# Up projection of a decoder layer: 18 seven-product steps instead of 16, four of them in each of two column groups

## The chip, the core and the metric

The kernel runs on one core of one Trainium2 chip. The metric is the device time of one execution in microseconds (us); lower is better. The core's engines work side by side, each with its own queue in fixed order: TensorE (PE, with its weight loads PEld) multiplies matrices into banks of PSUM, VectorE (DVE) and ScalarE (ACT) do elementwise work, GpSimd (POOL) and SyncE (SP) mostly issue transfers here. They wait for one another by semaphores.

## What is computed

One layer of a decoder trunk on 256 tokens of width 2048, all in float32: a mixer (mLSTM and attention heads), a gated feed-forward network, and a gated side input. The change concerns only the first product of the feed-forward network, the up projection:

```
h = rms_norm(x, ffn_norm_g)
u = h @ w_up                      # 256 x 2048 times 2048 x 11264
a, g = jnp.split(u, 2, axis=-1)   # 5632 columns each
a = causal_dwconv(a, conv_w, conv_b)
x = x + (jax.nn.gelu(a, approximate=False) * g) @ w_down
```

## The kernel before, in words

**One product.** TensorE takes each float32 operand as two rounded parts, a high part and a low rest, and forms high x high, high x low and low x high: three matmuls of 128 x 128 by 128 x 512 (`three`, lines 365 to 367). The left operand is the transposed, normed x (`x2`), kept in SBUF in both parts. The weights stream in from HBM once, and each block is split on the chip: ScalarE casts the high part (line 1296), VectorE subtracts it for the low one (line 1298).

**Column groups.** The up projection runs over 11 column groups q = 0 to 10 (`up_group`, line 1699), each of 512 columns of a and the same 512 of g. A group goes over 16 blocks k of 128 rows of the weights. A plain block ("p") is two halves of tokens by two halves of columns, four products, 12 matmuls, into four banks.

**Sevens.** Two blocks and the two halves of tokens make a 2 by 2 matrix product of blocks, which needs eight products as written and seven by the scheme of Strassen and Winograd. The kernel calls this a seven ("a" for the first pair of blocks of a group, "b" for the second). It comes as four units of 1, 2, 2 and 2 products (3, 6, 6, 6 matmuls, 21 instead of 24). For it VectorE forms four sums of weight halves ahead of the splits (lines 1743, 1744, 1754, 1755), and the sums of the left operand are made once for each pair of blocks (`up_sums`, line 1792) and kept in `S_up`. Four products go straight to the group's banks or to banks of their own (`pb`, tile name upP); at the last seven of a group four steps (lines 1765 to 1768) combine those banks into `z_up`, which is added to the group's rows later.

**The order of a group** is written out by hand as a string (`ORDERS`, line 48), one letter for each unit:

```
ORDERS = ("pppppp" "apapapap" "bpbbbp",
          *("pppppp" "apapapap" "pppp", "ppp" "apapapap" "bpbpbpb" "pp") * 4,
          *("pppppp" "apapapap" "pppp",) * 2)
```

So group 0 has two sevens, groups 1 to 8 have one and two in turn, groups 9 and 10 have one: 16 in all. `START[q]` is the index of a group's first unit.

**After a group.** Its four banks are scaled into `EZ` (`up_rows`, line 1154). Then, in the course of the next group: `up_turn` (line 1156) adds `z_up` (line 1161, twice) and transposes 32 x 32 squares into `Y` (line 202, twice), and 16 transfers on POOL and SP bring the squares back to `EZ` in place (line 208). `up_act` (line 1174) does ten steps: four scalings for the convolution (lines 1180 and 1183, ScalarE), two shifted sums (line 1187), GELU (line 1190), the gate (line 1193), the split into two parts (lines 158 and 159), and for some groups the left sums of the down projection (lines 470 to 474). `TURN_AT` and `ACT_AT` say behind which unit of the next group each step is queued, at the earliest.

**Lead and buffers** (`run_units`, line 1304). The queues of all engines are filled unit by unit. Before the matmuls of unit i are queued, loads are queued as long as a raw buffer is free, and splits for the units up to i + `AHEAD_UP` - 1 (4 ahead) as long as split buffers are free. There are eight raw buffers of 512 KB (raw0 to raw2, v0 to v4) and eight split buffers (four high, four low); a unit takes two split buffers, the first unit of a seven one. Buffers come back when TensorE has read them. The framework then lays down each engine's order from these queues and may move an instruction that has nothing to wait for ahead of one that has.

**Banks.** PSUM has four banks under each of two names, mm and aux. Even groups use mm for their rows and aux for their sevens; odd groups have aux for their rows and mm for their sevens.

Of the kernel before, what the change touches and what calls it, by code (L numbers as in the profile page):

```python
# [9 lines left out]
F32 = mybir.dt.float32  # L10
# [5 lines left out]
P = 128  # L16
S = 256
NT = S // P
# [6 lines left out]
KF = FF // P  # L25
# [8 lines left out]

BLK = 1024
RAW, PARTS = 3, 4
AHEAD_UP, AHEAD_LATE = 4, 6

SEVEN = (2, 4, 6, 8, 10, 12, 14, 16, 18)
FIRST = (0, 1, 2, 3, 5, 7, 4, 9, 6, 11, 8, 13, 10, 15, 12, 17, 14, 19, 16, 20, 18, 21)  # L40
# [4 lines left out]
FRONT = (8, 4, 4)  # L45
SEVENS_UP = 2
UP_K = (4, 5, 6, 7, 0, 1, 2, 3, 8, 9, 10, 11, 12, 13, 14, 15)
ORDERS = ("pppppp" "apapapap" "bpbbbp",
          *("pppppp" "apapapap" "pppp", "ppp" "apapapap" "bpbpbpb" "pp") * 4,
          *("pppppp" "apapapap" "pppp",) * 2)  # L50
START = [sum(map(len, ORDERS[:q])) for q in range(12)]
TURN_AT = (-1, -1, 0, 0)
GATE_ORDER = "ppppp" "apapapap" "bpbpbb" "p"
OUT_K = (8, 9, 10, 11, 12, 13, 14, 15, 0, 1, 2, 3, 4, 5, 6, 7)
OUT_ORDERS = ("pppp" "apapapap" "bpbpbpb" "p", "pp" "apapapa" "bpbpbb" "ppppp")
ACT_AT = (9, 10, 11, 12, 13, 14, 15, 16, 17, 18)


@with_exitstack
def layer_kernel(  # L60
# [29 lines left out]
    def f32(ap):  # L90
        return ap.bitcast(F32)
# [375 lines left out]
    def sums_of(u, f, t):  # L467

        a11, a12 = u[:, 0, 0:P], u[:, 1, 0:P]
        dve.tensor_sub(f[:, 1::2], u[:, 0].rearrange("p (i c) -> p i c", c=P), u[:, :, P:S])  # L470
        dve.tensor_sub(f[:, 0], f[:, 3], a11)
        dve.tensor_add(f[:, 2], a12, f[:, 0])
        act.copy(t[:, :, 0:P], f)
        dve.tensor_sub(t[:, :, P:256], f, f32(t[:, :, 0:P]))
# [30 lines left out]
    with mixers:  # L505
# [416 lines left out]
        at = len(blocks)  # L922
# [13 lines left out]
        def with_after(b, hook):  # L936
            fn = b.fn
            b.fn = lambda hi, lo: (fn(hi, lo), hook())
# [153 lines left out]
    with tc.tile_pool(name="ffn", bufs=1) as fp:  # L1092
# [4 lines left out]
        uB = fp.tile([P, 8, 512], F32R, tag="uB", name="uB")  # L1097
        uC = fp.tile([P, 8, 512], F32R, tag="uC", name="uC")
        S_up = [fp.tile([P, 4, 256], F32R, tag=f"u{42 - 2 * r}", name=f"S_up{r}") for r in range(SEVENS_UP)]
        spare_raws = {k: fp.tile([P, 2, BLK], F32, tag=k, name=f"{k}r") for k in ("u32", "u36")}  # L1100
        ends = {}

# [50 lines left out]

            act.activation(EZ[:, t, n * 512 : (n + 1) * 512], b, AF.Copy, scale=r2["t"][:, t : t + 1])

        def up_turn():

            y = Y.rearrange("p (t b c) -> p t b c", t=NT, b=4)

            def summed(t):  # L1160
                return lambda: dve.scalar_tensor_tensor(
                    out=EZ[:, t], in0=xs[:, 1, t * BLK : (t + 1) * BLK], scalar=r2["t"][:, t : t + 1], in1=EZ[:, t],
                    op0=ALU.mult, op1=ALU.add)

            def turned(t):
                def f():
                    square(y, t, 0, EZ[:, t])
                    if t == NT - 1:
                        with tc.issue_after(last["load"]):
                            move(y, Z, nc.sync)  # L1170
                return f
            return [f(t) for t in range(NT) for f in (summed, turned)]

        def up_act(q):

# [30 lines left out]

        late = {}
        now = [0]
        spaces = [f"raw{i}" for i in range(RAW)] + [f"{k}{i}" for k in ("hi", "lo") for i in range(PARTS)] + ["v0", "v1", "v2", "v3", "v4"]
        until = {"v0": 8, "v1": 8, "v2": 9, "v3": 9}  # L1210
        splits = (*spaces[RAW : RAW + 2 * PARTS], "w0", "w1", "w2", "w3")
        held, used = set(), {}
        for j in range(done[0] - PARTS, done[0]):
            used[f"hi{j % PARTS}"] = used[f"lo{j % PARTS}"] = used[f"raw{j % RAW}"] = len(used)
# [89 lines left out]
        def run_units(us, first_late, gate):  # L1304
            loaded = split = 0
            for i, u in enumerate(us):
                if i == first_late:
# [391 lines left out]
        def up_group(q):  # L1699
# [1 line left out]
            w = w_up[0].rearrange("(k p) (h c) -> k p h c", p=P, h=2)  # L1701
            st = {}

            n7 = "a" in ORDERS[q], "b" in ORDERS[q]
            first, n7 = 2 * sum(n7), sum(n7)
# [83 lines left out]
            kinds = {"p": iter(us), "a": iter(seven(0)), "b": iter(seven(1))}  # L1789
            return [next(kinds[c]) for c in ORDERS[q]]  # L1790

        def up_sums(r):
            k = UP_K[2 * r]
            f, d = (EZ[:, 0, i * 512 : (i + 1) * 512].rearrange("p (k c) -> p k c", c=256) for i in range(2))
            dve.tensor_add(f, f32(x2[:, k : k + 2, 0:256]), f32(x2[:, k : k + 2, 256:512]))
            sums_of(f, EZ[:, 1, 0:512].rearrange("p (i c) -> p i c", i=4), S_up[r])

        us = []
        for q in range(KF // 4):
# [2 lines left out]
        for i in range(4):  # L1802
            with_after(us[6 + 2 * i], between(lambda i=i: keep_x(4 + i)))
        with_after(us[3], between(lambda: r2.update(t=rstd_of(ssq2, "ffn"))))
        for r, i in enumerate((2, 9)):
            with_after(us[i], between(lambda r=r: up_sums(r)))
        for i, k0 in enumerate(range(8, KD, 2)):
            with_after(us[1 + i], behind(lambda k0=k0: transpose_x(x2, k0, g_ffn)))
# [16 lines left out]
            at = len(g_) // 2  # L1825
            us += g_[:at] + p_ + g_[at:]
        for q in range(KF // 4):
            for job, i in zip(up_turn(), TURN_AT if q < KF // 4 - 1 else (-1, 0, -1, 1)):
                with_after(us[START[q + 1] + i], between(job))
            for i, job in enumerate(up_act(q)):  # L1830
                if q < KF // 4 - 1:
                    with_after(us[START[q + 1] + ACT_AT[i]], between(job))
# [35 lines left out]
```

## Time and profile before

| | us |
|---|---|
| median of 3 runs | 1230.20 |
| lowest, highest | 1229.74, 1230.36 |
| the profiled execution | 1230.42 |
| span of its instructions | 1228.7 |

Busy time in the span: TensorE 1222.4, its weight loads 1029.6, VectorE 1010.1, ScalarE 757.2, GpSimd 179.7. The granted clock of TensorE is 0.999 on average.

A profile is one execution recorded by the hardware. Its page gives busy times, the chain of work that ended last and the costliest groups of instructions by line; the trace behind it answers questions: windows (busy time of each engine in a stretch), a timeline, groups by line and shape, and who waited for whom. "L1298" is line 1298 of the kernel. In a row such as "part<-raw" the tile written stands left and those read stand right. A number in square brackets is the idle time of the engine just before the instruction, with what ended it. Matmuls are pipelined, so single durations overlap and the distance from start to start is what one costs.

### The profile page before, as it was taken

To read this page: it belongs to the slowest core of one execution; us is meant where nothing else is said; L and a number is where in the kernel's file an instruction comes from. 1 tells how busy PE (TensorE), PEld (TensorE's weight loads), DVE (VectorE), ACT (ScalarE), POOL (GpSimd) and SP (SyncE) were. 2 spreads that over 40 slices of the span, in tenths; PEclk is the share of its full clock that TensorE was granted. 3 is DMA by queue.
4 is the path that set the end of the run, shared out by engine and by line. 5 is a ranking of instruction groups with operands and counts; after the bars stand their busy time and mean duration, and the time that the engine had idled before them with its cause. 6 is when DMAs were issued, how large, how long until landed. Compare 5 with 4: busy or idle time off the path is not lost.

```text
span 1228.7 us, 16419 instructions
## 1 busy us (share of the span) xinstructions
PE 1222.4 (99%) x5589; PEld 1029.6 (84%) x5589; DVE 1010.1 (82%) x1262; ACT 757.2 (62%) x1109; POOL 179.7 (15%) x331
## 2 busy tenths in 40 slices
PE   9999999999999999999999999999999999999998
PEld 7999988888888888888888888888888888888887
DVE  6788857675679989888998898998788999999773
ACT  7567545565655665766676676757657556556652
POOL 2011237243401401011101101110110000050000
PEclk9999999999999999999999999999999999999999
DMA  9566687676565787777687678756797896876570
GB/s 307 179 197 194 176 228 223 184 216 194 164 234 181 232 262 231 241 220 240 201 275 242 185 250 271 224 173 222 240 313 247 304 360 200 269 251 210 198 225 35
DMA packets 128869, 276.37 MB, mean 225 GB/s; under 512 B 14777, under 2 KB 26545, under 8 KB 128785
## 3 DMA queue, kind: packets, MB, share of 16 engines
q1 hardware_dynamic: 117392, 257.40, 65.9%
q0 software_dynamic: 11008, 17.76, 5.1%
q8 instruction: 44, 0.72, 0.2%
q14 instruction: 40, 0.33, 0.1%
q10 hardware_dynamic: 385, 0.16, 0.1%
HBM read 247.99 MB, written 8.93 MB: 209 GB/s over the span
## 4 chain that ended last, share of the span: by engine, by line
PE 99%; DMA 0%; SPq 0%; DVE 0%; ACT 0%; issue 0%; DVEq 0%
PE up L367 12%; PE up L365 12%; PE up L366 12%; PE tg L355 6%; PE tg L354 6%; PE tg L356 6%; PE pg L365 5%; PE pg L366 5%; PE pg L367 5%; PE dnP L1347 1%; PE dnP L1348 1%; PE dnP L1346 1%; PE upP L367 1%; PE upP L366 1%; PE upP L365 1%; PE gt L367 1%
## 5 line engine op out<-in xcount | busy, mean ns | idle before, releaser
L366 PE MATMUL up<-part,x2T 128*128 128x512 f32 x608 | 236.5, 389 | 0.0
L367 PE MATMUL up<-part,x2T 128*128 128x512 f32 x608 | 236.1, 390 | 0.0
L1296 ACT CAST part<-raw 128x1024 fp32r<-128x1024 f32 (+1 forms) x144 | 145.6, 1021 | 113.6 <-PE up L367 35.7
L300 DVE TENSOR_TENSOR lo<-raw,hi 128x1024 fp32r<-128x1024 f32 (+3 forms) x119 | 139.1, 1171 | 76.3 <-ACT hi L298 75.9
L365 PE MATMUL up<-part,x2T 128*128 128x512 f32 x608 | 185.9, 389 | 0.0
L1298 DVE TENSOR_TENSOR part<-raw,part 128x1024 fp32r<-128x1024 f32 (+1 forms) x140 | 164.1, 1179 | 23.4 <-ACT part L1296 17.1
L298 ACT CAST hi<-raw 128x1024 fp32r<-128x1024 f32 (+3 forms) x119 | 120.1, 1011 | 96.3 <-PE tg L356 44.9
L365 PEld LDWEIGHTS up<-part,x2T 128*128 128x128 f32 x608 | 114.2, 188 | 23.6
L366 PEld LDWEIGHTS up<-part,x2T 128*128 128x128 f32 x608 | 114.2, 188 | 23.6
L367 PEld LDWEIGHTS up<-part,x2T 128*128 128x128 f32 x608 | 114.0, 188 | 23.5
L356 PE MATMUL tg<-hi,hT 128*128 128x512 f32 x288 | 113.6, 395 | 0.0
L355 PE MATMUL tg<-lo,hT 128*128 128x512 f32 x288 | 113.3, 393 | 0.0
L354 PE MATMUL tg<-hi,hT 128*128 128x512 f32 x288 | 112.4, 396 | 0.0
L208 POOL DMA_DIRECT2D EZ<-Y x66 | 35.1, 539 | 364.3 <-issue 204.7
L1296 ACT CAST part<-u36r 128x1024 fp32r<-128x1024 f32 (+1 forms) x46 | 47.8, 1042 | 34.6 <-PE up L367 18.9
L1298 DVE TENSOR_TENSOR part<-u36r,part 128x1024 fp32r<-128x1024 f32 (+1 forms) x46 | 55.5, 1206 | 9.8 <-ACT part L1296 5.4
L355 PEld LDWEIGHTS tg<-lo,hT 128*128 128x128 f32 x288 | 54.1, 188 | 11.1 <-DVE lo L300 0.3
L356 PEld LDWEIGHTS tg<-hi,hT 128*128 128x128 f32 x288 | 54.1, 188 | 10.9
L354 PEld LDWEIGHTS tg<-hi,hT 128*128 128x128 f32 x288 | 53.8, 188 | 10.8
L1298 DVE TENSOR_TENSOR part<-u32r,part 128x1024 fp32r<-128x1024 f32 (+1 forms) x44 | 50.2, 1145 | 13.4 <-ACT part L1296 10.3
L1296 ACT CAST part<-u32r 128x1024 fp32r<-128x1024 f32 (+1 forms) x44 | 43.3, 991 | 22.7 <-PE up L367 9.0
L366 PE MATMUL pg<-lo,hT 128*128 128x430 f32 (+1 forms) x156 | 55.7, 357 | 0.0
(936 smaller groups left out, 2767.4 us busy)
## 6 DMA issues: line engine op xcount, KB each, us to landing
raw<-in_w_up_dram SPq DMA_DIRECT2D x78, 512.0 KB, 4.9
raw<-in_w_in_dram SPq DMA_DIRECT2D x71, 512.0 KB, 4.4
u36r<-in_w_up_dram SPq DMA_DIRECT2D x43, 512.0 KB, 5.2
raw<-in_w_down_dram SPq DMA_DIRECT2D x41, 512.0 KB, 5.6
u32r<-in_w_up_dram SPq DMA_DIRECT2D x34, 512.0 KB, 4.9
xs<-in_w_up_dram SPq DMA_DIRECT2D x21, 512.0 KB, 4.8
w2b<-in_w_down_dram SPq DMA_DIRECT2D x20, 512.0 KB, 5.9
raw<-in_w_out_dram SPq DMA_DIRECT2D x17, 512.0 KB, 4.8
```

The source lines that it names most:

```text
L208: (other if other and (4 * a + b) % 3 else pool).dma_start(out=c[32 * b : 32 * b + 32, a::4], in_=y[32 * a : 32 * a + 32, :, b])
L298: act.copy(hi, raw)
L300: dve.tensor_sub(lo, raw, f32(hi))
L354: pe.matmul(o, ah, hi[:, i, :], start=first, stop=False)
L355: pe.matmul(o, ah, lo[:, i, :], start=False, stop=False)
L356: pe.matmul(o, al, hi[:, i, :], start=False, stop=last)
L365: pe.matmul(o, ah, hi, start=start, stop=False)
L366: pe.matmul(o, ah, lo, start=False, stop=False)
L367: pe.matmul(o, al, hi, start=False, stop=stop)
L1296: act.copy(r32(hi), raw)
L1298: dve.tensor_sub(r32(lo), raw, hi)
L1346: pe.matmul(o, ah, hi, start=first, stop=False)
```

## The change

- The orders: group 0 keeps its two sevens. Groups 1 and 3 have none (16 plain units), groups 2 and 4 have four each ("a" to "d", 24 units, eight of them plain), groups 5 to 8 have one and two in turn as before, 9 and 10 have one. That is 18 sevens.
- Left sums: two more pairs of blocks get theirs, made in group 1 behind its units 3 and 5, and kept in a part of `uC`, which is used for other data only from group 6's results on.
- Four more split buffers, y0 to y3, in `uB`, usable for units from the seventh of group 1 to the eighth of group 5. `uB` is next written by the results of group 4.
- The lead is six units instead of four from unit 4 of group 1 to the end of group 4.
- `up_turn` leaves out its two additions of `z_up` behind a group without sevens; the steps of `up_act` are queued at other units in groups of 16 and of 24 units.

```diff
-AHEAD_UP, AHEAD_LATE = 4, 6
+AHEAD_UP, AHEAD_FOUR, AHEAD_LATE = 4, 6, 6
...
-ORDERS = ("pppppp" "apapapap" "bpbbbp",
-          *("pppppp" "apapapap" "pppp", "ppp" "apapapap" "bpbpbpb" "pp") * 4,
-          *("pppppp" "apapapap" "pppp",) * 2)
+NONE, ONE, TWO = "p" * 16, "pppppp" "apapapap" "pppp", "ppp" "apapapap" "bpbpbpb" "pp"
+FOUR = "p" "aapaap" "bbpbb" "ccpccp" "ddpdd" "p"
+ORDERS = ("pppppp" "apapapap" "bpbbbp", NONE, FOUR, NONE, FOUR, ONE, TWO, ONE, TWO, ONE, ONE)
...
-ACT_AT = (9, 10, 11, 12, 13, 14, 15, 16, 17, 18)
+ACT_AT = {16: (6, 7, 8, 9, 10, 11, 12, 13, 14, 15), 24: (8, 9, 11, 12, 14, 15, 17, 18, 20, 21)}
+ACT_ELSE = (9, 10, 11, 12, 13, 14, 15, 16, 17, 18)
...
+        S_up += [uC[:, 2 * i : 2 * i + 2].rearrange("p k (x c) -> p (k x) c", c=256) for i in range(2)]
...
-        def up_turn():
+        def up_turn(with_z):
...
-            return [f(t) for t in range(NT) for f in (summed, turned)]
+            return [f(t) if f is turned or with_z else (lambda: None) for t in range(NT) for f in (summed, turned)]
...
-        splits = (*spaces[RAW : RAW + 2 * PARTS], "w0", "w1", "w2", "w3")
+        splits = (*spaces[RAW : RAW + 2 * PARTS], "y0", "y1", "y2", "y3", "w0", "w1", "w2", "w3")
...
+                if t[0] == "y":
+                    return START[1] + 6 <= j < START[5] + 8
...
+            elif tag[0] == "y":
+                v = f32(uB[:, 2 * i : 2 * i + 2]).rearrange("p k c -> p (k c)")
...
-                ahead = AHEAD_LATE if i >= first_late else AHEAD_UP
+                ahead = AHEAD_LATE if i >= first_late else AHEAD_FOUR if START[1] + 4 <= i < START[5] else AHEAD_UP
...
-        for r, i in enumerate((2, 9)):
+        for r, i in enumerate((2, 9, START[1] + 3, START[1] + 5)):
             with_after(us[i], between(lambda r=r: up_sums(r)))
...
-            for job, i in zip(up_turn(), TURN_AT if q < KF // 4 - 1 else (-1, 0, -1, 1)):
+            for job, i in zip(up_turn("a" in ORDERS[q]), TURN_AT if q < KF // 4 - 1 else (-1, 0, -1, 1)):
```

More of the change, by code (lines that the diff above doesn't have):

```diff
@@ L1208, in layer_kernel @@
         now = [0]
-        spaces = [f"raw{i}" for i in range(RAW)] + [f"{k}{i}" for k in ("hi", "lo") for i in range(PARTS)] + ["v0", "v1", "v2", "v3", "v4"]
+        spaces = [f"raw{i}" for i in range(RAW)] + [f"{k}{i}" for k in ("hi", "lo") for i in range(PARTS)] + ["v0", "v1", "v2", "v3", "v4", "y0", "y1", "y2", "y3"]
         until = {"v0": 8, "v1": 8, "v2": 9, "v3": 9}
-        splits = (*spaces[RAW : RAW + 2 * PARTS], "w0", "w1", "w2", "w3")
+        splits = (*spaces[RAW : RAW + 2 * PARTS], "y0", "y1", "y2", "y3", "w0", "w1", "w2", "w3")
         held, used = set(), {}
@@ L1702, in up_group @@
             st = {}
-            n7 = "a" in ORDERS[q], "b" in ORDERS[q]
-            first, n7 = 2 * sum(n7), sum(n7)
+            n7 = len(set(ORDERS[q]) - {"p"})
+            first = 2 * n7
             def left(k, t):
@@ L1788, in up_group @@
             us = [unit(j) for j in range(first, KD)]
-            kinds = {"p": iter(us), "a": iter(seven(0)), "b": iter(seven(1))}
+            kinds = {"p": iter(us), **{c: iter(seven(r)) for r, c in enumerate("abcd"[:n7])}}
             return [next(kinds[c]) for c in ORDERS[q]]
@@ L1793, in up_sums @@
             k = UP_K[2 * r]
-            f, d = (EZ[:, 0, i * 512 : (i + 1) * 512].rearrange("p (k c) -> p k c", c=256) for i in range(2))
-            dve.tensor_add(f, f32(x2[:, k : k + 2, 0:256]), f32(x2[:, k : k + 2, 256:512]))
-            sums_of(f, EZ[:, 1, 0:512].rearrange("p (i c) -> p i c", i=4), S_up[r])
+            if r < 2:
+                w, f = EZ[:, 0], EZ[:, 1]
+            else:
+                v = fp.tile([P, BLK], F32, tag="pT", name="Sd_up")
+                w, f = v[:, 0:512], v[:, 512:1024]
+            d = w[:, 0:512].rearrange("p (k c) -> p k c", c=256)
+            dve.tensor_add(d, f32(x2[:, k : k + 2, 0:256]), f32(x2[:, k : k + 2, 256:512]))
+            sums_of(d, f[:, 0:512].rearrange("p (i c) -> p i c", i=4), S_up[r])
         us = []
@@ L1831, in layer_kernel @@
                 if q < KF // 4 - 1:
-                    with_after(us[START[q + 1] + ACT_AT[i]], between(job))
+                    at = ACT_AT.get(len(ORDERS[q + 1]), ACT_ELSE)
+                    with_after(us[START[q + 1] + at[i]], between(job))
                 else:
```

## The prediction

> **What bounds the kernel now.** I read the page first: the shares of the engines, then the chain that ended last.
>
> ```profile
> span 1228.7 us, 16419 instructions
> ...
> PE 1222.4 (99%) x5589; PEld 1029.6 (84%) x5589; DVE 1010.1 (82%) x1262; ACT 757.2 (62%) x1109; POOL 179.7 (15%) x331
> ...
> PE 99%; DMA 0%; SPq 0%; DVE 0%; ACT 0%; issue 0%; DVEq 0%
> ```
>
> TensorE carries the span, and the chain that ended last is TensorE for 99% of it. The change lies wholly in the up projection, so the next view is the table of windows there. The timeline shows the up projection's matmuls from 425 to 897 us; one window over it, then one window for each column group, cut where the next group's first matmul starts. The numbers of a row are the window's length, then the busy time (and count) of PE, PEld, DVE, ACT and POOL, then the granted clock, the DMA share and GB/s. First the whole stage:
>
> ```profile
> 425.00:897.00 472.00, 472.00 (x2091) 390.87 (x2090) 415.06 (x445) 315.86 (x430) 37.11 (x69) 1.00 0.74 233
> ```
>
> Then the four groups with two sevens (columns q = 2, 4, 6, 8):
>
> ```profile
> 513.98:556.14 42.16, 42.16 (x188) 34.92 (x186) 37.31 (x40) 29.50 (x40) 3.16 (x6) 1.00 0.71 220
> ...
> 768.98:811.14 42.16, 42.16 (x188) 34.92 (x186) 39.19 (x44) 30.36 (x43) 3.76 (x7) 1.00 0.67 211
> sum 168.64, PE 168.64 PEld 139.69 DVE 153.59 ACT 119.38 POOL 14.43; mean PE 42.16 PEld 34.92 DVE 38.40 ACT 29.85 POOL 3.61
> ```
>
> And four of the groups with one seven (q = 1, 3, 5, 7):
>
> ```profile
> 471.14:513.98 42.84, 42.84 (x191) 35.48 (x189) 36.23 (x35) 27.45 (x36) 3.21 (x6) 1.00 0.80 255
> ...
> 726.14:768.98 42.84, 42.84 (x191) 35.48 (x189) 38.26 (x40) 28.50 (x39) 3.73 (x7) 1.00 0.77 239
> sum 171.36, PE 171.36 PEld 141.94 DVE 149.69 ACT 111.95 POOL 14.47; mean PE 42.84 PEld 35.48 DVE 37.42 ACT 27.99 POOL 3.62
> ```
>
> TensorE is never idle in the stage, and its clock is granted in full. A group with two sevens has 62 products of three matmuls, one with one seven 63. The windows are 42.16 and 42.84 us long: 186 and 189 matmuls at 0.2267 us, and 0.68 us for the one product between them. So in this stage time is the count of matmuls and nothing else, until some engine makes TensorE wait. VectorE is the engine that could: it is busy 38.4 of 42.2 us where there are two sevens.
>
> **The change part by part.**
>
> *Matmuls.* The old orders hold 2 + 4 x (1 + 2) + 2 x 1 = 16 sevens, the new 2 + 0 + 4 + 0 + 4 + 1 + 2 + 1 + 2 + 1 + 1 = 18. Each replaces 24 matmuls by 21, so 6 matmuls go: 6 x 0.2267 = 1.36 us, all of it on the path that sets the end. Nothing is added on TensorE: the sums of the left operand are made on VectorE and ScalarE.
>
> The Trainium skill (Perfetto Trace Analysis, "Identifying the Most-Contended Engine") says that matmul busy time does not tell how near TensorE is to its limit and that weight-load busy time does. By that rule TensorE would stand at 34.92 of 42.16, some 83%, and six products less could be worth nothing. The trace disagrees: three matmuls less shorten a group by just their own 0.68 us.
>
> *VectorE's work.* How long its instructions take from start to start when nothing holds them, from the timeline of VectorE at the end of the first group:
>
> ```profile
> 460.75 0.68 DVE L1298 TENSOR_TENSOR part<-raw,part 128x512 fp32r<-128x512 f32 x1
> 461.47 0.69 DVE L1743 TENSOR_TENSOR raw<-raw 128x512 f32<-128x512 f32 x1
> 462.20 0.69 DVE L1744 TENSOR_TENSOR raw<-u32r,raw 128x512 f32<-128x512 f32 x1
> ...
> 463.65 0.69 DVE L1755 TENSOR_TENSOR u32r<-u32r 128x512 f32<-128x512 f32 x1
> 464.26 1.22 DVE L1298 TENSOR_TENSOR part<-raw,part 128x1024 fp32r<-128x1024 f32 x1
> 465.40 1.22 DVE L1298 TENSOR_TENSOR part<-u36r,part 128x1024 fp32r<-128x1024 f32 x1
> 466.53 1.22 DVE L1298 TENSOR_TENSOR part<-u32r,part 128x1024 fp32r<-128x1024 f32 x1
> 467.67 2.58 DVE L1298 TENSOR_TENSOR part<-raw,part 128x1024 fp32r<-128x1024 f32 x2
> 470.43 0.69 DVE L1766 TENSOR_TENSOR xs<-upP,xs 128x512 f32<-128x512 f32 x1 [0.18 <-PE upP L367]
> 471.16 0.69 DVE L1767 TENSOR_TENSOR xs<-upP,xs 128x512 f32<-128x512 f32 x1
> ...
> 473.11 1.22 DVE L1768 TENSOR_TENSOR xs<-upP,xs 128x1024 f32<-128x1024 f32 x1
> 474.25 1.22 DVE L1298 TENSOR_TENSOR part<-u32r,part 128x1024 fp32r<-128x1024 f32 x1
> 475.38 2.48 DVE L1161 SCALAR_TENSOR_TENSOR EZ<-xs,rstd_ffn,EZ 128x1024 f32<-128x1024 f32 x2
> 477.77 2.37 DVE L202 STREAM_TRANSPOSE Y<-EZ 128x1024 f32<-128x1024 f32 x2
> ```
>
> A full split, like any full-width step, is 1.14 us (464.26 to 465.40), a half-width step 0.72. A seven costs one half split, four half-width sums and three full splits: 460.75 to 467.67, 6.92 us; the two plain blocks that it replaces cost 2.28. Combining the sevens of a group costs 0.73 + 0.73 + 1.14 = 2.60 (L1766 to L1768), adding the result to the rows 2.39 (L1161, twice), turning them 2.3.
>
> A group of four is a group of two with two more sevens, four plain blocks fewer, and without the L1161 pair, since the group before it has no sevens: 38.40 + 13.84 - 4.56 - 2.39 = 45.3 us of VectorE, against 180 x 0.2267 = 40.8 us of TensorE. **It is short by 4.5 us.** A group of none is one of one without its seven and its combining: 37.42 - 6.92 + 2.28 - 2.60 = 30.2 us against 192 x 0.2267 = 43.5. The first of them also makes the two new left sums, each by five steps:
>
> ```profile
> L474 DVE TENSOR_TENSOR S_up<-EZ,S_up 128x512 fp32r<-128x512 f32 x2 | 1.4, 686 | 0.7 <-ACT S_up L473 0.7
> L1795 DVE TENSOR_TENSOR EZ<-x2T 128x512 f32<-128x512 f32 x2 | 1.4, 683 | 0.0
> L470 DVE TENSOR_TENSOR EZ<-EZ 128x256 f32<-128x256 f32 x2 | 0.8, 420 | 0.0
> L471 DVE TENSOR_TENSOR EZ<-EZ 128x128 f32<-128x128 f32 x2 | 0.6, 290 | 0.0
> L472 DVE TENSOR_TENSOR EZ<-EZ 128x128 f32<-128x128 f32 x2 | 0.6, 284 | 0.0
> ```
>
> That is 2.36 us each, 4.7 in all, which makes 34.9 of 43.5: hidden, with over 8 us to spare. Pair by pair (none, then four) VectorE has 75 to 80 of TensorE's 84.3 us, so all fits if the lead carries the 4.5 us.
>
> *The lead.* With four blocks of lead VectorE runs out of buffers, not of time, in a group of two:
>
> ```profile
> 535.99 1.22 DVE L1298 TENSOR_TENSOR part<-u36r,part 128x1024 fp32r<-128x1024 f32 x1 [3.72 <-PE up L367]
> ```
>
> And a cast on ScalarE, which goes ahead of each split, takes 1.05 us:
>
> ```profile
> L1296 ACT CAST part<-raw 128x1024 fp32r<-128x1024 f32 x84 | 87.8, 1050 | 66.1 <-PE up L367 33.3 <-PE up L366 9.0 <-PE upP L367 4.6
> ```
>
> VectorE, in the upper row, sat 3.72 us until TensorE gave one back. Six blocks at the head of a group of four (p a a p a a) are 12 + 3 + 6 + 12 + 6 + 6 = 45 matmuls, 10.2 us; with TensorE at work on the first, the other five are 33 matmuls, 7.5 us. That carries 4.5 us with 3 to spare, if it is full at the start, as the spare of a group of none allows. The tight place is the tail, where the lead shrinks and work comes in between. Count from the group's first matmul. Block 16 (the third of c) needs the buffers of block 10, free at 78 matmuls, 17.7 us; its cast takes about 1.1 and its two sums (1.44) are done before. From there to block 23 (the last of d) VectorE has two full splits of c with one pair of sums still to do, two plain, d's 6.92, and the two shifts and the gating of the group before (3 x 1.14): 1.14 + 2.58 + 2.28 + 6.92 + 3.42 = 16.3 us, so 17.7 + 1.1 + 16.3 = 35.1. TensorE asks for block 23 at 162 matmuls, 36.7 us. **Margin 1.6 us.** So I take no wait, and 1.6 us as what may go wrong without being seen. A split into one of the four new buffers is costed as any other; they are an existing tile that is idle until later groups.
>
> *Queues.* The two turns stay at the group's head, and with them the 16 moves that they release, ten on SP's queue ahead of the next loads. The scaling that needs the moves comes earlier: after block 9 of the group (66 matmuls, 15.0 us) where a group of two has it after block 10 (93 matmuls, 21.1 us). In the second group of two, which begins at 598.98, it went like this, on VectorE, SP's queue and ScalarE:
>
> ```profile
> 607.52 1.24 DVE L202 STREAM_TRANSPOSE Y<-EZ 128x1024 f32<-128x1024 f32 x1
> ...
> 608.78 6.50 SPq L208 DMA_DIRECT2D EZ<-Y  x10
> ...
> 618.33 0.60 ACT L1180 ACTIVATE xs<-EZ,cT 128x256 f32<-128x256 f32 x1
> ```
>
> The second turn ended 9.8 us behind the group's start, the last move was issued at 16.3, and the scaling began at 19.4. In a group of four the two L1161 steps between the turns are gone, so the turns can end by some 5 us and the moves be issued by 12; I take no wait. If the turns come as late as here, ScalarE waits some 4 us, with the casts of later blocks queued behind it. ScalarE has room for the work itself: 29.85 of 42.16 us with two sevens, and two more sevens cast two half and six full widths more and their plain blocks four fewer, about 3 us. Loads are as many as before.
>
> *The end of a group of four.* Only one plain block follows the last seven, and the next group writes to the banks that hold its sums. The first group ends in the same way: there the third combining step ran from 473.11 to 474.33, 3.2 us after the next group's first matmul (471.14), and TensorE was busy without a break. So I take nothing here.
>
> **The sum.** 1230.42 us, the profiled execution, less 1.36, is 1229.06. The median of the runs is 1230.20, so against it **1228.84 us**. The gain is 0.11%; about 0.2%, or 2.46 us, is what a measurement of this kernel can tell from no change.
>
> **The rivals.**
>
> *The gain goes into the change of banks.* After the last product of d the combining needs 2.60 us; TensorE can go on for the 12 matmuls of the last block and the 6 of the next group that use the banks freed first, 4.08 us. With the group's pending parts step (1.14) and one more split (1.14) ahead of it, 4.9 us: 0.8 us of wait in each of the two groups, 1.6 in all, and the time is 1230.4. With the left sums and a second split as well the wait is up to 3.6 each. For it: VectorE is at its busiest there. Against it: the first group's end, above.
>
> *ScalarE waits for the moves, TensorE starves in the tail, and the kernel is slower.* The scaling has waited for its moves once, for the last group, behind the up projection (timeline of ScalarE):
>
> ```profile
> 921.69 0.60 ACT L1180 ACTIVATE xs<-EZ,cT 128x256 f32<-128x256 f32 x1 [4.81 <-DMA EZ<-Y]
> ```
>
> In the stage itself (groups by line there) nothing idled ahead of its 40 instructions:
>
> ```profile
> L1180 ACT ACTIVATE xs<-EZ,cT 128x256 f32<-128x256 f32 x40 | 23.9, 597 | 0.0
> ```
>
> If it waits so long in each group of four, the casts and VectorE's splits behind it come 4.8 us late, just ahead of the stretch where the margin is 1.6: 3.2 us show, twice, and 6.4 - 1.36 = 5.0 us slower is 1235.2. It decides from 3.5 us lost in each group on (3.5 - 1.6 = 1.9, twice, less 1.36 is 2.46). For it: the scaling stands 6 us earlier than before and its moves only some 4 us. Against it: casts may stand ahead of it in the queue while the moves have not landed, and the 0.0 of the stage itself.
>
> The Trainium skill (TensorE: Matmul & The Clock Gate, "HAM oscillation — how this bites in real kernels") warns that TensorE drops to half its clock after an idle gap of some 3.4 us. No run here shows it in this stage, where the clock is 1.00 and nothing idles.
>
> *The products removed are not worth their time*, the rule of the weight loads above: 1230.2. The 0.68 us between the two kinds of window speaks against it.
>
> **How the numbers follow.** No wait, 1228.8: 0.64. Banks, 1230.4: 0.20. Starved, 1235.2: 0.11. Nothing gained, 1230.2: 0.03. Something unforeseen saves over an additional 1.1 us: 0.02, as no row shows a wait of TensorE's to be saved. So faster 0.02, same 0.64 + 0.20 + 0.03 = 0.87, slower 0.11. The range reaches from the forecast less the spread of the runs shown (0.6 us), 1228.2, to the banks' case with 1.4 us of wait in each group instead of 0.8 (of at most 3.6), 1231.6. It leaves out the starved case and the worst of the banks.
>
> **What would show it.** Right: groups of none 43.5 us long and groups of four 40.8 in the windows, TensorE without idle time in them, VectorE idle for the lack of buffers in the groups of none and near 45 us of work for each group of four (some of it in the next window). The banks: idle TensorE just behind the start of groups 3 and 5. Starved: idle TensorE before the blocks of d, with VectorE at work or waiting for a cast. The prediction is wrong if TensorE idles over 1 us in the stage, or if its other stages change in length.

## The result and the profile after

The changed kernel takes **1236.41 us** (median of 6 runs, 1235.35 to 1238.00) against 1229.90 for the kernel before on the same chip (6 runs, 1229.71 to 1230.36): a ratio of 1.0051 [1.0040, 1.0061], slower by half a per cent where a gain of 0.11% was forecast. The profiled execution of after is the fastest of its six, 1235.35 us; what follows accounts for the 4.93 us between it and the profiled execution of before (1230.42). The other runs of after lie up to 2.65 us higher, and no trace of them exists.

The page of after, the same lines as were shown of before:

```profile
span 1233.6 us, 16403 instructions
...
PE 1225.1 (99%) x5583; PEld 1029.6 (83%) x5583; DVE 1012.9 (82%) x1274; ACT 759.4 (62%) x1113; POOL 178.2 (14%) x331
...
PE 93%; DVE 2%; DMA 1%; ACT 1%; issue 1%; SPq 1%; DVEq 0%; ACTq 0%
```

The six matmuls are gone (5589 to 5583), and still TensorE's busy time went up, by 2.7 us. The chain that ended last now leaves TensorE for 6% of its length, by way of VectorE, ScalarE and the DMA. So there are waits, and the question is where. The table of windows of after, for groups 1 to 5 and group 10 (cut at the same matmul of each group, in the order of TensorE, as in the prediction; columns as there):

```profile
470.54:518.56 48.02, 46.06 (x194) 36.95 (x192) 41.37 (x46) 32.40 (x44) 3.21 (x6) 0.96 0.72 238
518.56:559.36 40.80, 40.80 (x182) 33.80 (x180) 37.63 (x41) 29.29 (x40) 3.16 (x6) 1.00 0.72 221
559.36:603.45 44.09, 43.81 (x193) 35.97 (x192) 36.73 (x39) 28.64 (x40) 3.78 (x7) 1.00 0.74 237
603.45:644.25 40.80, 40.80 (x181) 33.80 (x180) 38.74 (x45) 29.75 (x41) 3.73 (x7) 1.00 0.74 235
644.25:687.66 43.41, 43.13 (x190) 35.41 (x189) 38.09 (x40) 27.96 (x39) 3.78 (x7) 1.00 0.74 231
...
857.66:901.75 44.09, 43.45 (x190) 35.33 (x189) 35.21 (x37) 27.20 (x38) 3.74 (x7) 1.00 0.75 243
```

By count of matmuls the lengths should be 43.52 for a group of none, 40.80 for one of four, 42.84 for one seven. The two groups of four, rows two and four, are exactly 40.80 with TensorE never idle. The loss is elsewhere: 4.50 us in group 1, 0.57 in group 3, 0.57 in group 5, 1.25 in group 10, 6.89 in all. Less the 1.36 us of the matmuls, and less 0.60 us by which the stage began earlier in this execution (424.65 instead of 425.25), that is the 4.93. The rest of the kernel, from the end of the stage to the last matmul, is 327.39 us in both traces.

Two thirds of the loss sit in group 1, a plain group that the change was to make easy. TensorE there, on the timeline:

```profile
470.99 0.39 PE L368 MATMUL up<-part,x2T 128*128 128x512 f32 x1
471.79 0.50 PE L366 MATMUL up<-part,x2T 128*128 128x512 f32 x1 [0.41 <-ACT part L1302]
473.84 0.50 PE L367 MATMUL up<-part,x2T 128*128 128x512 f32 x1 [1.55 <-DVE part L1304]
...
475.54 0.63 PE L366 MATMUL up<-part,x2T 128*128 128x512 f32 x1
475.96 0.63 PE L367 MATMUL up<-part,x2T 128*128 128x512 f32 x1
```

At the second block of the group (unit 21) TensorE waits for the block's high part from ScalarE and then for its low part from VectorE. From start to start, less 0.23 for the matmul itself, 0.57 and 1.82 us are lost, 2.40. A little later the matmuls are 0.42 us apart instead of 0.227. The windows show why:

```profile
474.00:476.00 2.00, 2.00 (x7) 1.35 (x8) 2.00 (x4) 2.00 (x4) 0.00 (x0) 0.72 1.01 344
476.00:478.00 2.00, 2.00 (x6) 1.62 (x5) 2.00 (x4) 0.87 (x1) 0.00 (x0) 0.50 0.84 251
478.00:480.00 2.00, 2.00 (x9) 1.61 (x9) 2.00 (x3) 0.00 (x0) 0.00 (x0) 0.93 0.78 241
```

The granted clock falls to one half. The missing shares, 2.00 x (0.28 + 0.50 + 0.07), are 1.70 us. Idle and slow clock make 4.10 of the 4.50. Of the rest, 0.11 is the matmul that starts 0.34 behind the one of 473.84, and some 0.2 a second short wait, at 486.69, for a low part that VectorE ended at 486.64. The higher busy time of TensorE is mostly these slow matmuls: it is busy for 46.06 us in this group, where 43.52 are needed.

Who came late is read on ScalarE, in after:

```profile
465.44 1.05 ACT L1302 CAST part<-raw 128x1024 fp32r<-128x1024 f32 x1
466.38 0.58 ACT L1771 COPY xs<-upP 128x512 f32<-128x512 f32 x1
469.73 1.05 ACT L1302 CAST uB<-xs 128x1024 fp32r<-128x1024 f32 x1 [2.77 <-DMA xs<-in_w_up_dram]
470.69 1.05 ACT L1302 CAST part<-raw 128x1024 fp32r<-128x1024 f32 x1
471.63 1.83 ACT L1156 ACTIVATE EZ<-up,rstd_ffn 128x512 f32<-128x512 f32 x3
```

and in before:

```profile
466.99 0.57 ACT L1765 COPY xs<-upP 128x512 f32<-128x512 f32 x1
467.94 1.06 ACT L1296 CAST part<-raw 128x1024 fp32r<-128x1024 f32 x1 [0.38 <-PE upP L367]
468.90 1.84 ACT L1154 ACTIVATE EZ<-up,rstd_ffn 128x512 f32<-128x512 f32 x3
```

The third row of after is new: a cast into `uB`, the tile of the four new buffers. It waited 2.77 us for a load of weights, and the cast behind it, at 467.94 in before, ran at 470.69. On SP's queue the load it waited for is the first of five issued in a row:

```profile
465.41 0.54 SPq L1279 DMA_DIRECT2D xs<-in_w_up_dram  x1
...
468.32 0.54 SPq L1279 DMA_DIRECT2D raw<-in_w_up_dram  x1
```

From its issue to the start of the cast passed 4.3 us. The load was not late: in before it was issued at 465.91, in a trace that runs 0.60 behind. New is that a cast waited for it. The order in which the two built programs hold ScalarE's instructions says which block it is (position, line, instruction; the first number in `part21_0` is that of the unit):

```
after   398 L1771 COPY xs_84<-upP1_4306          before  398 L1765 COPY xs_84<-upP1_4306
        399 L1302 CAST uB_4103<-xs_84                    399 L1296 CAST part21_0_4481<-raw21_0_4349
        400 L1302 CAST part21_0_4481<-raw21_0_4349       400 L1154 ACTIVATE EZ_4109<-up00_4141,rstd_ffn_4241
        401 L1156 ACTIVATE EZ_4109<-up00_4141,rstd_ffn_4241
```

The cast into `uB` is that of unit 26, the first allowed into a new buffer. The kernel's code writes its split while unit 23 is worked on, five casts behind that of unit 21; the framework that orders the instructions moved it ahead of all five (and unit 27's ahead of unit 22's). ScalarE executes in the order it is given, so everything behind the cast waited too. VectorE had the same order:

```profile
470.82 1.23 DVE L1304 TENSOR_TENSOR uB<-xs,uB 128x1024 fp32r<-128x1024 f32 x1 [2.53 <-ACT uB L1302]
471.96 0.69 DVE L1806 TENSOR_TENSOR Sd_up<-x2T 128x512 f32<-128x512 f32 x1
472.56 1.22 DVE L1304 TENSOR_TENSOR part<-raw,part 128x1024 fp32r<-128x1024 f32 x1
```

Idle for 2.53 us, then the far block's split, a left-sum step, and only then unit 21's low part, done at 473.78. TensorE wanted it two matmuls behind the row of 470.99, at 471.45, so it is 2.33 us late, nearly all of the 2.40 lost above. In before the same low part was done at 470.25 (467.67 + 2.58, a row of the prediction), and TensorE used it here:

```profile
472.05 0.39 PE L366 MATMUL up<-part,x2T 128*128 128x512 f32 x1
```

That is a spare of 1.8 us, which no part of the prediction looked at.

At the start of groups 3 and 5 the wait is 0.28 us each, for a first cast that stood behind scalings on ScalarE. In group 10, at 890.38, it is 0.59 us:

```profile
884.80 1.05 ACT L1302 CAST part<-xs 128x1024 fp32r<-128x1024 f32 x1 [2.17 <-DMA xs<-in_w_up_dram]
...
889.29 1.03 ACT L1302 CAST part<-raw 128x1024 fp32r<-128x1024 f32 x1
```

In the built program the lower cast is that of unit 208, which TensorE waits for; it stands behind the cast of unit 209 and three scalings, and units 204 and 203, 206 and 205 are swapped in the same way. The upper one, of unit 207 and in its place, waits 2.17 us for its weights. None of the new buffers is in use there; the framework's order came out otherwise than in before, where the corresponding casts stand in the order of units.

### The profile page after: what moved, and what is told of

It is laid out like the page before. It is cut to its first block, busy times and chain, and to the rows that moved or that the text cites. A ratio compares the mean times of both kernels' runs of the same rounds, so it can differ in the third digit from the quotient of the medians.

```text
span 1233.6 us, 16403 instructions
## 1 busy us (share of the span) xinstructions
PE 1225.1 (99%) x5583; PEld 1029.6 (83%) x5583; DVE 1012.9 (82%) x1274; ACT 759.4 (62%) x1113; POOL 178.2 (14%) x331
## 4 chain that ended last, share of the span: by engine, by line
PE 93%; DVE 2%; DMA 1%; ACT 1%; issue 1%; SPq 1%; DVEq 0%; ACTq 0%
PE up L367 10%; PE up L366 10%; PE up L368 10%; PE tg L355 6%; PE tg L356 6%; PE tg L357 6%; PE pg L366 5%; PE pg L367 5%; PE pg L368 5%; PE dnP L1354 1%; PE dnP L1352 1%; PE dnP L1353 1%; PE upP L367 1%; PE upP L366 1%; PE upP L368 1%
## 5 line engine op out<-in xcount | busy, mean ns | idle before, releaser
L367 PE MATMUL up<-part,x2T 128*128 128x512 f32 x523 | 204.4, 391 | 1.6 <-DVE part L1304 1.6
L368 PE MATMUL up<-part,x2T 128*128 128x512 f32 x524 | 204.0, 391 | 0.0
L1302 ACT CAST part<-raw 128x1024 fp32r<-128x1024 f32 (+1 forms) x139 | 139.0, 1010 | 103.1 <-PE up L367 20.3
L1304 DVE TENSOR_TENSOR part<-raw,part 128x1024 fp32r<-128x1024 f32 (+1 forms) x134 | 155.3, 1167 | 35.9 <-ACT part L1302 27.4
L366 PE MATMUL up<-part,x2T 128*128 128x512 f32 x524 | 171.5, 392 | 1.3 <-ACT part L1302 1.3
L366 PEld LDWEIGHTS up<-part,x2T 128*128 128x128 f32 x524 | 98.8, 189 | 23.3 <-ACT part L1302 2.5
L367 PEld LDWEIGHTS up<-part,x2T 128*128 128x128 f32 x523 | 98.5, 188 | 23.0 <-DVE part L1304 2.7
L368 PEld LDWEIGHTS up<-part,x2T 128*128 128x128 f32 x524 | 98.5, 188 | 20.2
L1302 ACT CAST part<-u36r 128x1024 fp32r<-128x1024 f32 x41 | 42.9, 1050 | 28.3 <-PE up L368 17.0
L368 PE MATMUL pg<-hi,hT 128*128 128x430 f32 (+1 forms) x156 | 55.6, 356 | 0.0
L1304 DVE TENSOR_TENSOR part<-u36r,part 128x1024 fp32r<-128x1024 f32 x39 | 47.5, 1220 | 7.6 <-ACT part L1302 6.9
L1302 ACT CAST part<-u32r 128x1024 fp32r<-128x1024 f32 (+1 forms) x35 | 34.4, 988 | 23.9 <-PE up L368 12.6
```

Of the source, the lines that this page charges most:

```text
L366: pe.matmul(o, ah, hi, start=start, stop=False)
L367: pe.matmul(o, ah, lo, start=False, stop=False)
L368: pe.matmul(o, al, hi, start=False, stop=stop)
L1302: act.copy(r32(hi), raw)
L1304: dve.tensor_sub(r32(lo), raw, hi)
```

## The experiments

The theory, called "early cast" below: the framework lets units 26 and 27 into the new buffers ahead of nearer blocks, and their wait for weights costs the 4.5 us. The rivals: VectorE simply has too much work in the groups of four; or the two new left sums in group 1 are in the way. Each kernel was timed beside the kernel before on its chip; the ratio is to that.

**The order of the new buffers alone (e1_order).** A split that takes a new buffer is queued behind the split of the block before it; nothing else is changed.

```diff
-                        us[split].split(split)
+                        if any(t[0] == "y" for t in free_of(split, True)[: us[split].needs]):
+                            with tc.issue_after(last["hi"]), tc.issue_after(last["lo"]):
+                                us[split].split(split)
+                        else:
+                            us[split].split(split)
```

> The changed kernel, with one thing more: a split into one of the four new buffers is queued on ScalarE and VectorE behind the split of the unit before it. Orders, buffers, lead and left sums as in the change. Theory 'early cast' (on ScalarE the cast of unit 26 into a new buffer stands ahead of the cast of unit 21, waits 2.8 us for its weights and keeps TensorE waiting, which then runs at half its clock): the idle time and the half clock at 471 us go, 4.3 us of the 6.9 lost in the stage, so 1236.4 - 4.4 = 1232.0 us, 1231.3 to 1232.8. Theory 'too much work for VectorE' (groups of four and the lead): nothing changes, 1236. Theory 'left sums' (the two new left sums stand ahead of the split that TensorE waits for): at most 0.6 us less, about 1236.

1229.91 us against 1230.58, 0.9992 [0.9983, 1.0001]. The slowdown is gone altogether, and the time lies below the range expected. The windows of groups 1 to 4:

```profile
470.88:514.40 43.52, 43.52 (x194) 36.05 (x193) 38.34 (x43) 29.29 (x39) 3.21 (x6) 1.00 0.77 263
514.40:555.84 41.44, 41.32 (x181) 33.63 (x180) 38.10 (x41) 30.73 (x42) 3.16 (x6) 1.00 0.71 208
555.84:599.36 43.52, 43.52 (x193) 36.04 (x192) 37.04 (x40) 28.15 (x39) 3.78 (x7) 1.00 0.75 250
599.36:640.16 40.80, 40.80 (x181) 33.78 (x180) 36.73 (x42) 28.56 (x40) 3.74 (x7) 1.00 0.71 217
```

Group 1 is at its 43.52, and the clock is whole. The pairs near 890 went too, which the expectation had not counted on. What is left is 0.64 us in group 2, at 542, in the tail where the prediction had its margin of 1.6, and 0.35 at the start of group 5.

**The new buffers from group 2 on (e2_late_y).**

```diff
-                    return START[1] + 6 <= j < START[5] + 8
+                    return START[2] <= j < START[5] + 8
```

> The changed kernel with the four new buffers open from unit 36 on (first of group 2) instead of unit 26. Theory 'early cast': no cast can go early at the border of groups 0 and 1, the same 4.3 us go, 1232.0 us (1231.3 to 1232.8), with TensorE busy through 460 to 490 us. Theory 'too much work for VectorE': less lead in group 1, so the same or slower, 1236 to 1237. Theory 'left sums': about 1236.

1230.45 against 1230.58, 0.9994 [0.9985, 1.0003]; no cast stands ahead of unit 21's, and TensorE loses nothing at 471 or near 890, so this too is better than expected. The lead of six blocks is not what hurt: e1_order keeps it together with the buffers, and units 26 and 27 are queued three units ahead, which the lead of four of before allows as well.

**The left sums six units later (e3_sums_late).**

```diff
-        for r, i in enumerate((2, 9, START[1] + 3, START[1] + 5)):
+        for r, i in enumerate((2, 9, START[1] + 9, START[1] + 11)):
```

> The changed kernel with the two new left sums made behind units 9 and 11 of group 1 instead of 3 and 5. Theory 'early cast': the early cast still stands ahead of unit 21's, so the wait and the half clock at 471 us stay, 1235.5 to 1237. Theory 'left sums': VectorE is free at the border of the groups, 2 us and the half clock go, 1232 to 1233.5. Theory 'too much work for VectorE': 1236.

1236.00, 1.0036 [1.0023, 1.0050]. The wait at 471 stays, from start to start 1.94 us where after lost 2.40; with the matmuls behind it 2.20 us are lost there, since this time the clock did not fall. A new wait of 1.86 and 0.46 us at 543 to 546, with half clock behind it, brings the total back to the one expected, which is luck. So the left sums make little of the wait at 471; why there is one at 543 was not followed up.

**Before's orders, with only the new buffers and the lead (e4_lead_only).** Sixteen sevens, and the two left sums of before.

```diff
-ORDERS = ("pppppp" "apapapap" "bpbbbp", NONE, FOUR, NONE, FOUR, ONE, TWO, ONE, TWO, ONE, ONE)
+ORDERS = ("pppppp" "apapapap" "bpbbbp", *(ONE, TWO) * 4, ONE, ONE)
...
-        for r, i in enumerate((2, 9, START[1] + 3, START[1] + 5)):
+        for r, i in enumerate((2, 9)):
```

> The orders of the kernel before (16 sevens, none of the groups of four or of none) with the change's four new buffers and its lead of six, without the two new left sums. Theory 'early cast': the sevens do not matter, an early cast into a new buffer stands ahead of unit 21's here too, so TensorE idles near 471 us and runs at half its clock behind it: 1230.0 + 2 to 5 = 1232 to 1235 us. Theory 'too much work for VectorE': more lead at the old load, 1230.0 us. Theory 'left sums': 1230.0 us.

1233.27 against 1230.58, 1.0019 [1.0010, 1.0028]: slower without one more seven. On ScalarE:

```profile
470.27 0.62 ACT L1302 CAST uB<-xs 128x512 fp32r<-128x512 f32 x1 [2.67 <-DMA xs<-in_w_up_dram]
470.80 1.05 ACT L1302 CAST part<-raw 128x1024 fp32r<-128x1024 f32 x1
```

The same cast in the same place. 1.25 us are lost at 471 to 474, without a fall of the clock, and 1.25 in group 10, where the pairs are swapped here too.

**The orders without buffers and lead (e5_no_lead).**

```diff
-AHEAD_UP, AHEAD_FOUR, AHEAD_LATE = 4, 6, 6
+AHEAD_UP, AHEAD_FOUR, AHEAD_LATE = 4, 4, 6
...
-                    return START[1] + 6 <= j < START[5] + 8
+                    return False
```

> The changed kernel with its orders and left sums, but without the four new buffers and with the lead of four. Theory 'early cast': no free buffer lets a cast go early at the border of groups 0 and 1, so nothing idles near 471 us. The forecast's running sum: block 16 of a group of four then waits for the buffers of block 12 instead of 10, 2.7 us later, against a margin of 1.6, and the first sevens come too close as well, so TensorE idles in groups 2 and 4 by 2 to 4 us each; 1229.1 + 4 to 8 = 1233 to 1237 us. If groups of four need no lead, 1229 to 1230.

1240.10 against 1230.44, 1.0076 [1.0063, 1.0089], above the range expected. Nothing idles at 471, but the two groups of four are now short:

```profile
514.20:558.68 44.48, 41.92 (x181) 33.55 (x180) 42.56 (x48) 31.23 (x43) 3.16 (x6) 1.00 0.67 202
602.27:647.79 45.52, 43.06 (x181) 34.30 (x180) 43.66 (x52) 31.74 (x44) 3.74 (x7) 0.96 0.69 211
```

3.68 and 4.72 us over 40.80, near the 4.5 us that the prediction found VectorE short by. With the lead and its buffers they are 40.80: together these carry them.

**All splits in a fixed order (e6_all_order), and the same on before (e7_before_order).** The two lines of e1_order around every split of the stage ahead of the last few, instead of those into new buffers.

```diff
+                        if 0 < split < first_late:
+                            with tc.issue_after(last["hi"]), tc.issue_after(last["lo"]):
```

> The changed kernel with every split of the up projection queued behind the split of the unit before it, on ScalarE and VectorE. Theory 'early cast', widened: also the 1.2 us of TensorE near 890 us come from casts that stand out of the order of units (there 209 ahead of 208), so no wait is left at 471 or 890, and what is left are the 0.5 us at the end of each group of four: the forecast, 1229.1 us (1228.7 to 1230.0), 0.05 to 0.15 per cent faster than before. If the fixed order costs more than the swaps did, VectorE idles ahead of casts and it is 1231 or more.

> The kernel before with every split of the up projection queued behind the split of the unit before it: the control for the run with the changed kernel. In the kernel before, TensorE never idles in this stage, so there is nothing to win: 1230.2 us (within 0.1 per cent). If the fixed order has a price of its own, it shows here.

1270.60, 1.0322 [1.0308, 1.0336], and 1259.89, 1.0237 [1.0223, 1.0251]: the expectations failed, by 41 and 30 us. VectorE's waits for casts, in before and then in e7_before_order, over the same stretch:

```profile
DVE part L1298 <- ACT part L1296: 34.1, 38, 3.9
```

```profile
DVE part L1298 <- ACT part L1296: 69.5, 65, 7.1
```

They double. That splits now stand behind all the sums and casts of a seven ahead of them, whether ready or not, is how I read it. So the freedom to move splits is worth some 30 us to the kernel before, and what hurt the change most is that same freedom at one spot.

**Only units 26 and 27 in order (e10_two_casts).** e1_order with a narrower condition.

```diff
-                        if any(t[0] == "y" for t in free_of(split, True)[: us[split].needs]):
+                        if split < 28 and any(t[0] == "y" for t in free_of(split, True)[: us[split].needs]):
```

> The changed kernel with only the splits of units 26 and 27, the first two that go into new buffers, queued behind the split before them; all others as the change has them. Theory 'early cast': these two carry the whole loss at 471 us (4.3 us). What stays are about 1 us at the ends of the groups of four and, as casts 209 and 208 are swapped here as in the changed kernel, 1.2 us near 890: 1229.1 + 2.2 = 1231.3 us (1230.3 to 1232.2), that is 5 us less than the change. Theory 'too much work for VectorE': 1236.

1231.31 against 1230.17, 1.0010 [1.0001, 1.0019]. Against after's 1236.41 the places of two splits carry some 5 us. Its waits on TensorE are the small ones only, groups 3, 5 and 10:

```profile
PE up L366 <- ACT part L1302: 0.7, 2, 0.4
PE up L366 <- ACT uB L1302: 0.3, 1, 0.3
```

**One older spare buffer later as well (e11_no_v4).** `v4`, a buffer of before that is also usable from unit 26 on, is kept back until group 2.

```diff
-                    return j >= 26 and (not late or j < late["x"])
+                    return j >= START[2] and (not late or j < late["x"])
```

> The changed kernel with one raw buffer (v4, the part of xs that unit 26 loads into) closed until group 2. The casts of units 26 and 27 still stand early, but 26 now behind 21 and ahead of 22, 27 ahead of 24, and from weights that other buffers hold. If an early cast hurts because it waits for its weights ahead of a cast that TensorE needs at once, little is left of the loss at 471 us: under 1 us there and no half clock, 1230 to 1232.5 us with what else waits. If an early cast hurts wherever it stands, 2 us or more are left there: 1233 to 1236.

1233.92 against 1230.17, 1.0023 [1.0013, 1.0034]. Unit 26's cast now stands between those of 21 and 22, and I had taken its weights to be there by then. They were not:

```profile
473.99 1.05 ACT L1302 CAST uB<-u36r 128x1024 fp32r<-128x1024 f32 x1 [3.84 <-DMA u36r<-in_w_up_dram]
474.94 1.04 ACT L1302 CAST part<-u36r 128x1024 fp32r<-128x1024 f32 x1
```

3.84 us of wait, 1.25 and 1.18 us of idle TensorE, half clock behind them, some 4.4 us in all. The second of the two is a wait for a combining step (`xs`, L1774) that stood behind the same split on VectorE. The time is the one expected if an early cast hurts wherever it stands, but this run doesn't show that, since the cast waited here too: the place changed, the mechanism did not.

**How long a pause the clock bears (e8_probe).** In before, ten splits repeat their low-part subtraction three to seven times more; no number of the result changes.

```diff
-            dve.tensor_sub(r32(lo), raw, hi)
+            for _ in range(1 + again[0]):
+                dve.tensor_sub(r32(lo), raw, hi)
```

> The kernel before with ten probes: in groups 1 to 10 the low part of one plain unit is subtracted 4, 5, 6, 7, 8, 4, 5, 6, 7, 8 times instead of once, which changes no number, and keeps VectorE 1.14 us longer for each. With 2 to 4 us of lead TensorE should idle by 0 to 1, 1 to 2, 2 to 3, 3 to 4, 4 to 6 us. It shows from which idle time on the granted clock falls behind it. The rule of the Trainium skill's page on TensorE: from some 3.4 us on, so in about four of ten. As read from the changed kernel's wait at 471 us (2.05 and 0.8 us from start to start, half the clock for 3.3 us behind it): from about 2 us on, in about six of ten.

One run, 1306.86 us. Nine of the ten pauses, with 1.97 to 7.9 us of idle time each, were followed by half clock, where six of ten were expected at most. The three with the least idle time differ (TensorE's timeline, then the windows behind each):

```profile
479.84 0.39 PE L368 MATMUL up<-part,x2T 128*128 128x512 f32 x1
482.20 0.50 PE L368 MATMUL upP<-part,x2T 128*128 128x512 f32 x1 [1.97 <-ACT part L1301]
...
541.65 0.50 PE L368 MATMUL upP<-part,x2T 128*128 128x512 f32 x1 [1.79 <-ACT part L1301]
543.28 0.50 PE L369 MATMUL up<-part,x2T 128*128 128x512 f32 x1 [1.12 <-DVE part L1304]
...
745.61 0.51 PE L368 MATMUL upP<-part,x2T 128*128 128x512 f32 x1 [1.79 <-ACT part L1301]
747.24 0.50 PE L369 MATMUL up<-part,x2T 128*128 128x512 f32 x1 [1.13 <-DVE part L1304]
```

```profile
482.30:486.00 3.70, 3.70 (x10) 2.88 (x11) 3.70 (x4) 0.38 (x1) 0.00 (x0) 0.55 0.87 265
543.40:547.00 3.60, 3.60 (x10) 2.81 (x11) 3.46 (x6) 1.45 (x4) 0.00 (x0) 0.60 0.87 282
747.40:751.00 3.60, 3.60 (x16) 2.96 (x17) 3.50 (x5) 2.08 (x5) 0.00 (x0) 1.00 0.87 287
```

1.97 us in one piece brought the clock down to 0.55. Of two pauses that are alike, 1.79 and 1.12 or 1.13 us with a matmul between, one brought it down to 0.60 and the other left it at 1.00. So the length of a pause alone does not decide.

**A version with both spots changed (e9_two_last).** e1_order, with the last four splits of group 10 in unit order as well, and the plain block between the sevens a and b moved to the end of the group, so that two plain blocks follow d.

```diff
-FOUR = "p" "aapaap" "bbpbb" "ccpccp" "ddpdd" "p"
+FOUR = "p" "aapaa" "bbpbb" "ccpcc" "p" "ddpdd" "pp"
...
+                        if START[10] + 14 <= split < first_late or any(t[0] == "y" for t in free_of(split, True)[: us[split].needs]):
```

> The run e1_order (splits into new buffers queued behind the split before them) with two more edits: the order of a group of four puts its last two plain units behind the last seven instead of one, and the last four splits of group 10 are queued in the order of units. No early cast, twice the cover at the end of a group of four, no swap of casts near 890 us. If the 0.9 us that TensorE still idles in e1_order came from the ends of the groups of four, it falls to 0 to 0.4: 1229.0 us, 0.05 to 0.15 per cent faster than before. If it came from VectorE's lead running out ahead of the last seven, it stays or grows, since a plain unit less stands ahead of d: 1230 to 1231.5.

1229.43 against 1230.17, 0.9991 [0.9982, 1.0000]. Groups 1 and 2 are clean; some 0.34 us at the end of group 4 and 0.55 in group 10, at 886, are lost, more than the 0 to 0.4 expected. The windows of groups 2 and 4:

```profile
514.39:555.19 40.80, 40.80 (x182) 33.78 (x180) 38.53 (x41) 30.85 (x42) 3.16 (x6) 1.00 0.70 207
598.71:639.80 41.09, 41.06 (x181) 33.71 (x180) 37.92 (x45) 31.08 (x43) 3.75 (x7) 1.00 0.73 226
```

It has the lowest median of all the kernels run, 0.74 us below before; the interval reaches no change, so it is not told apart from it.

## Why the prediction was wrong

**The step that failed** is in "The lead": "A split into one of the four new buffers is costed as any other; they are an existing tile that is idle until later groups." The work of such a split is that of any other, 1.05 and 1.23 us. Its place is not. The buffers of the old splits are given back by TensorE, and so a split into them can't stand far ahead; one into an idle tile waits for nothing but its weights, and the framework put it five casts forward. That the lack of an earlier reader is what let it go there is argued from the order, and fits e2_late_y, where the same buffers come into use in group 2 and no cast runs ahead. What it cost is measured: 4.50 us in group 1, nearly all at 471, of which 2.40 are idle and 1.70 half clock. It is gone in e1_order and e10_two_casts, and there again in e4_lead_only (1.25) and e11_no_v4 (some 4.4).

The failure has a second half. The spare was counted at one place, the tail of a group of four (1.6 us). The border of groups 0 and 1 had 1.8 us, and was never looked at, since nothing there seemed to change; the row of VectorE that begins it, 467.67 with 2.58, stood in the prediction, the matmul that ends it did not.

**The six matmuls** are worth their time: the groups of four are 40.80 long, 1.36 less than a group of two, which has six matmuls more, and the groups of none, once undisturbed, 43.52.

**VectorE's 4.5 us and the lead** held: with the lead the groups of four lose nothing in after, without it 3.68 and 4.72. Pair by pair (none, then four) VectorE was busy 79.0 and 75.5 us, where 75 to 80 were forecast. The margin of 1.6 was thin, as said: a little other order took it up in e1_order (0.64 us at 542) and e3_sums_late.

**The queues.** In the groups of four no wait for the moves showed on TensorE, as forecast. But the rival that I gave 0.11, "ScalarE waits for the moves, TensorE starves in the tail", had the right mechanism with another transfer: ScalarE at the head of its queue waiting for a DMA, casts behind it, and, by luck, a price near (1235.2 against 1236.4 measured, but by another sum and in another group). I asked that question of the moves alone, and not of the loads of weights, on which every cast depends.

The Trainium skill (Perfetto Trace Analysis, "Tensor Engine Instruction (MATMUL, LD_WEIGHTS)") says that ScalarE and VectorE are strictly first in, first out. The trace agrees: unit 21's cast and three scalings started only behind the cast that had waited 2.77 us, where in before they ran 2.7 us earlier.

**The end of a group of four.** I took nothing; 0.57 us was lost in each of groups 3 and 5, short of the 0.8 of the rival of the banks, and by a cast that stood behind scalings, not by the combining. With the 1.25 of group 10, which the edit doesn't touch, that is 2.39 us, more than the 1.36 to be gained: e10_two_casts, where only the early casts are put right, comes out at 1231.31. So the gain itself is seen in the windows of the groups, and in no run's time clear of noise.

**The range** ended at 1231.6, 4.8 below the median. It held the cost of everything that the change adds, and no cost of the order in which it would be put; the chance of slower, 0.11, was too small for the same reason.

## What to carry to other kernels

Where a framework orders the instructions, a new buffer is also a new freedom: a step that has nothing to wait for but a transfer can be put at the head of an engine's queue, and nearer work waits behind it. When a change adds buffers or lead, ask of each engine's queue what can now move ahead, on which load it waits, and where the spare was thinnest before, outside the edited groups too. Tie only those steps to their neighbours; tying all of them cost 30 us here.

## What the runs showed of the hardware

A short pause of TensorE can cost well more than its length: 2.40 us idle drew 1.70 us of half clock in after. The clock was halved there for about 3.4 us (1.1 + 2.0 + 0.3 by the three windows). In e5_no_lead, behind waits of 0.89, 0.76 and 0.78 us from 642 on with matmuls between, it stayed halved for some 6.8 us (the granted clock is 0.50 from 645.5 to 651.0, 0.66 in the 1.5 us ahead of that and 0.84 in the 1.0 behind). The Trainium skill (TensorE: Matmul & The Clock Gate, "What's actually happening") gives about 3.4 us both for the idle window behind which the clock falls and for the busy one behind which it comes back, and says that the window runs freely. The second figure agrees with the 3.4 us in after; the 6.8 of e5_no_lead are twice it. The first doesn't, as a threshold for a pause: the clock fell after 1.97 us in one piece (e8_probe), after 0.41 + 1.55 with a matmul between (after), after 1.25 + 1.18 (e11_no_v4) and after 1.79 + 1.12 (e8_probe, at 543), and not after 1.79 + 1.13 (e8_probe, at 747). A window that runs freely could make two such equal pauses differ; what decides between them was not tried and stays open.
